# Attention items in the order of query blocks 2, 0, 3, 1, one input chunk turned later, and the last item's transposes moved between out_proj's products

## The chip, the cores and the metric

The kernel runs on one core of one Trainium2 chip. The core has five engines with a queue of instructions each: TensorE (PE in the profile; its weight loads are a row of their own, PEld), VectorE (DVE), ScalarE (ACT), GpSimd (POOL) and SyncE (SP). The metric is the device time of one execution in microseconds (us).

## The reference, cut to what matters

Input x is 512 tokens by 1024 features, float32. Layer A is a gated short convolution and a squared-ReLU MLP; from its output one shared key/value side is projected. Layer B is sparse attention with three branches and a second MLP; a final RMS norm ends it.

```
h = rms_norm(x, norm_mix[0]); b, c, u = split(h @ w_in, 3)
x = x + (b * conv3(c * u)) @ w_out                       # layer A
x = x + square(relu(rms_norm(x) @ w1)) @ w2
k_cmp, v_cmp, k_sel, v_sel, k_win, v_win = shared_kv(rms_norm(x, kv_norm))
q, gates = split(rms_norm(x, norm_mix[1]) @ w_qg)        # layer B
for each query block of 128 tokens, each of 16 heads in 4 groups:
    o_b = softmax(q @ k_b.T + bias, causal) @ v_b        # b = compressed, selected, window
    o = gates[0] * o_c + gates[1] * o_s + gates[2] * o_w
x = x + o @ w_o
x = x + square(relu(rms_norm(x) @ w1)) @ w2
return rms_norm(x, final_norm)
```

With 512 tokens the selected and the window branch both see all earlier keys: block qb of four attends to 128 * (qb + 1) keys in each. The compressed branch has 31 keys.

## The kernel before, in words

Activations lie with features on the partitions, 8 chunks of 128 features by 512 tokens. A product in float32 accuracy is made of three float16 products: every operand is split into a high and a low half (mm3, lines 355 to 358: high by high, high by low, low by high). Weights come from HBM in pieces of up to 1024 columns into a staging tile (wst, 3 buffers), ACT makes the high half (L202), DVE the low half (L203); next_piece (line 215) hands out a piece, and ahead and ahead_fine convert the pieces that follow it. Loads are issued on SP's queue, a piece's load when a staging buffer is free again.

**Start.** x is loaded in four parts of 1, 1, 2 and 2 chunks, with the first weight pieces between them; the last two chunks follow within the first loop. x_chunk (lines 385 to 395) turns a chunk: four transposes on PE (L389) into bank d (even chunks) or e (odd), split by ACT (L303, x0h) and DVE (L304, x0l), and a copy to X by DVE (L394). Seven and later five products on an idle tile (L246) keep PE busy until data is there. The loop from line 418 on works with one weight piece per chunk: chunk c's products for three outputs (pc, pu, pb: two banks each, three products for each, so 18 products of 128x512) and then chunk c + 2 is turned. Ahead of the loop chunks 0 and 1 are turned.

**Attention.** PSUM has banks a, b, c (two of each) and d, e (one of each). An item is a Full (group g, query block qb, branch br, some heads) or a Cmp (the compressed branch for two groups). A Full of block 0 has four heads of 128 keys, of block 1 two of 256, of block 2 one of 384, of block 3 one of 512. So a group has 2, 4, 8 and 8 items in its four blocks, 22 in all, and there are 88 Full and 8 Cmp. An item's stages:

- st0: scores on PE into a bank b (L985, L986); per head, DVE adds the bias and finds the extreme (L993, with a read of the accumulator), ACT takes the exponential (L995, with a read of the sum).
- st1: the probabilities are turned on PE into a bank c (L1001); ACT makes their high half (L1004).
- st2: DVE makes the low half (L1007).
- st3: values on PE into bank d, one bank for all heads and both branches of a block (L1020 to L1022). With a block's last item DVE takes the reciprocal of the sums (L1027), multiplies by the gates (L1028) and scales bank d into o_t (L938); POOL adds the branches up (L940, L943; add_parts).
- st4: where a block has all three branches, finish turns it on PE into a bank c (L954) and ACT and DVE split it into ot (L377, L379).

The loop over i at line 1151 emits st0 of item i, then some background work, then st1 to st4 of items i - 2, i - 3, i - 4 and i - 6. The background generator holds the products that attention still needs (raw keys, queries of groups 1 to 3, the phi network) and out_proj(0), output projection for groups 0 and 1; it is drawn by a credit of 0.65 to 1.03 us an item. Queries of a group are split by ACT (L774) and POOL (L775), four heads. Items stand group by group (line 1128), in a group by blocks 0, 1, 2, 3. Cmp(0, 0) to Cmp(0, 3) stand behind the items 9 to 12 of group 2, Cmp(1, 0), (1, 1), (1, 3), (1, 2) behind the items 3, 7, 11, 15 of group 3. A Cmp whose two groups have both their Full parts is scaled and finished for both at once, else for each by itself.

When the loop ends, the rest of the background runs, then out_proj(2) for groups 2 and 3. Its products over chunks 0 and 1 belong to group 2, those over chunks 2 and 3 to group 3. With early = 2 the first two of the four pairs of outputs do their products over chunks 0 and 1 first. The second MLP follows.

The framework that builds the kernel orders each engine's instructions by itself from the dependences and the order in which they were emitted; issue_after ties a block's instructions on an engine behind a given one.

Of the kernel before, what the change touches and what calls it, by code (L numbers as in the profile page):

```python
# [48 lines left out]
def body(ctx, tc, x, rel_bias, norm_mix, norm_mlp, mlp_w1, mlp_w2, a_w_in, a_conv_w, a_w_out,  # L49
# [176 lines left out]
    def drain(gen):  # L226
        for _ in gen:
            pass
# [126 lines left out]
    def mm3(ps, w, xs, start, stop):  # L355
        PE.matmul(ps, w[0], xs[0], start=start, stop=False)  # L356
        PE.matmul(ps, w[0], xs[1], start=False, stop=False)  # L357
        PE.matmul(ps, w[1], xs[0], start=False, stop=stop)  # L358

    def pair(xs, ps, kn=8, mid=None):  # L360

# [22 lines left out]
    xs = new_split(wk[0], "x0")  # L384

    def x_chunk(c):
        p = bank("de"[c % 2])
        for t in range(4):
            last = PE.transpose(p[:, t * 128:(t + 1) * 128], xt[t][:, c * 128:(c + 1) * 128], ident)  # L389
        if c == 0:  # L390
            with tc.issue_after(last.ins):
                keep_busy(5)
        hi = split_gain(xs, c, p, "mix0")
        DVE.tensor_copy(X[:, c], p)  # L394
        return hi
# [10 lines left out]
    for p in range(4):  # L406
        pc, pu, pb = [], [], []
        if p == 0:
            for dst in (pc, pu, pb):
                dst += [acc(), acc()]  # L410

            def first_pairs(dst, w, c):
                part = 1 if dst is pc else 2 if dst is pu else 0
                for m in range(2):
                    mm3(dst[m], [u[:, part, m * 128:(m + 1) * 128] for u in w], [u[:, c] for u in xs],
                        c == 0, c == 7)

            hi = [x_chunk(0), x_chunk(1)]
            for c in range(6):
                with tc.issue_after(hi[0].ins) if c == 0 else nullcontext():  # L420
                    w = next_piece()
                if c == 0:
                    load_x(6, 8)
                if c == 3:
                    later_vectors()
                for dst in (pc, pu, pb):
                    first_pairs(dst, w, c)
                with tc.issue_after(hi[c + 1].ins):
# [199 lines left out]
    with pool("attn") as ap:  # L628
# [245 lines left out]
        ss2 = SumSq()  # L874
        xm = None

        def out_proj(g, early=0):

            ws, pos_ = [], []

            def products(p, chunks, cv=iter(())):
                for c in chunks:
                    for m in range(2):
                        mm3(pos_[p][m], [u[:, c, m * 128:(m + 1) * 128] for u in ws[p]],
                            [u[:, 2 * g + c] for u in ot], c == 0, c == 3)
                        next(cv, None)
                        yield 0.65

            for p in range(early):
                ws.append(next_piece())  # L890
                pos_.append([abank(), abank()])
                drain(products(p, (0, 1)))
            for p in range(4):
                if p >= early:
                    ws.append(next_piece())
                    pos_.append([abank(), abank()])
                po = pos_[p]
# [44 lines left out]
                for b in range(nb):  # L942
                    POOL.tensor_tensor(dst, dst, t[:, b], op=OP.add)  # L943

        def finish(g, n, qb):

            nonlocal ot
            if ot is None:
                o16 = ap.tile([128, 2, 8, S], F16, name="big", bufs=1)
                ot = (o16[:, 0], o16[:, 1])  # L950
            p = bank("c")
            for j in range(n):
                for i in range(2):
                    PE.transpose(p[:, (2 * j + i) * 128:(2 * j + i + 1) * 128],  # L954
# [10 lines left out]
        class Full:  # L965
# [65 lines left out]
                else:  # L1031
                    self.last = False

            def st4(self):
                if self.last:
                    finish(self.g, 1, self.qb)

        class Cmp:

# [73 lines left out]
            n = max(1, 4 >> qb) if qb < 2 else 1  # L1113
            return [tuple(range(h, h + n)) for h in range(0, 4, n)]

        def full(g):
            return [Full(g, qb, br, hs) for qb in range(4) for br in range(2) for hs in heads_of(qb)]


        def mixed(rest, cmps):  # L1120
# [5 lines left out]
            return out_  # L1126

        items = full(0) + full(1)
        items += mixed(full(2), {9 + qb: Cmp(0, qb) for qb in range(4)})
        items += mixed(full(3), {3: Cmp(1, 0), 7: Cmp(1, 1), 11: Cmp(1, 3), 15: Cmp(1, 2)})  # L1130
        at_item = {11: lambda: load_T(1), 35: lambda: load_T(2), 60: lambda: load_T(3)}
        copy_at = {16: 1, 40: 2, 65: 3}
# [15 lines left out]

        lead = {1: 2, 2: 3, 3: 4, 4: 6}
        credit = 3.0  # L1150
        for i in range(len(items) + 6):
            if i < len(items):
                for k in items[i].need():
                    while k not in done:
# [12 lines left out]
                    credit -= u or 0.1  # L1167
            for s in (1, 2, 3, 4):
                j = i - lead[s]
                if 0 <= j < len(items):  # L1170
                    getattr(items[j], f"st{s}")()
        for _ in bg:
            pass
        lead_in[0] = True
        xm = new_split(work, "xs")
        drain(out_proj(2, 2))
    xs = xm
    ss = ss2

# [156 lines left out]
```

## Time and profile before

| | us |
|---|---|
| median of 3 runs | 1118.34 (1118.34 to 1118.35) |
| the profiled execution | 1118.71 |
| its span, first to last instruction | 1116.9 |
| PE busy in the span | 1091.2 |
| DVE busy | 870.1 |
| ACT busy | 571.0 |
| POOL busy | 58.8 |

The profile is of one execution. A row of a group names line, engine, operation, output<-inputs by the program's names, shapes and count; then the busy time in us, the mean of one in ns, and the idle time of the engine just before them with what ended it. A row of the timeline has the start in us, the duration, engine, line and operation, and in brackets the idle time before it. Matmuls are pipelined: rows overlap, and one's duration is longer than the distance to the next. A row of waits reads "engine line <- what it waited for: us in total, times, longest".

### The profile page before, as it was taken

The page shows a single profiled execution, that of the slowest core. Times are in us where ns is not written, and L with a number is a line of the kernel's source. Part 1 is how long each engine was busy: PE and PEld are TensorE (multiplying, and loading weights), DVE is VectorE, ACT ScalarE, POOL GpSimd, SP SyncE. Part 2 cuts the span into 40 slices and gives each one's busy share as a digit, 9 for nine tenths or more (in the row PEclk, how much of TensorE's full clock was granted, in tenths as well). Part 3 has the DMA queues.
Part 4 walks back from the last instruction along what each step waited for, and adds up shares of the span by engine and source line. Part 5 has one row for each costly group of instructions (what it writes and reads, how often), then busy time and mean ns, then how long its engine had stood idle before and what let it go on. Part 6 is the DMA issues. An engine that isn't in the chain of part 4 may idle for free.

```text
span 1116.9 us, 20043 instructions
## 1 busy us (share of the span) xinstructions
PE 1091.2 (98%) x7960; PEld 693.6 (62%) x7960; DVE 870.1 (78%) x1624; ACT 571.0 (51%) x921; POOL 58.8 (5%) x73
## 2 busy tenths in 40 slices
PE   9999999999999999999998999899999999999996
PEld 4444444446885448875867676675444788445895
DVE  5755466987998667969589879997998798865775
ACT  4532244545343444447678786875655434342352
POOL 1000000000000000000102021311000000000020
PEclk9999999999999999999999999999999999999998
DMA  6433335543333333313333232111653333330321
GB/s 214 127 102 94 113 95 151 149 117 113 114 115 116 104 101 103 106 31 110 116 90 123 84 111 77 39 40 57 180 160 109 105 112 111 114 94 1 95 76 76
DMA packets 149709, 115.75 MB, mean 104 GB/s; under 512 B 8700, under 2 KB 146640, under 8 KB 149616
## 3 DMA queue, kind: packets, MB, share of 16 engines
q1 hardware_dynamic: 146624, 108.88, 32.1%
q10 hardware_dynamic: 2608, 4.97, 1.4%
q8 instruction: 62, 1.02, 0.4%
q0 software_dynamic: 384, 0.63, 0.2%
q14 instruction: 31, 0.25, 0.1%
HBM read 110.22 MB, written 2.14 MB: 101 GB/s over the span
## 4 chain that ended last, share of the span: by engine, by line
PE 89%; DVE 4%; ACT 3%; issue 1%; POOL 1%; DMA 1%; SPq 0%; DVEq 0%; ACTq 0%; POOLq 0%
PE c L572 8%; PE a L572 8%; PE a L356 6%; PE a L357 6%; PE a L358 6%; PE b L358 6%; PE b L357 6%; PE b L356 6%; PE c L357 6%; PE c L356 6%; PE c L358 6%; PE b L572 6%; PE d L572 4%; PE c L1001 2%; PE e L572 2%
## 5 line engine op out<-in xcount | busy, mean ns | idle before, releaser
L202 ACT ACTIVATE whi<-wst 128x1024 f16<-128x1024 f32 (+3 forms) x173 | 144.6, 850 | 180.3 <-PE b L357 64.8
L203 DVE SCALAR_TENSOR_TENSOR wlo<-wst,whi 128x1024 f16<-128x1024 f32 (+3 forms) x173 | 170.9, 996 | 41.7 <-ACT whi L202 41.3
L572 PEld LDWEIGHTS <-whi 128*128 128x128 f16 x1792 | 175.4, 98 | 20.6
L358 PEld LDWEIGHTS <-wlo 128*128 128x128 f16 x1024 | 100.1, 98 | 112.4 <-DVE wlo L203 0.6
L356 PEld LDWEIGHTS <-whi 128*128 128x128 f16 x1024 | 100.4, 98 | 109.6 <-issue 2.7
L357 PEld LDWEIGHTS <-whi 128*128 128x128 f16 x1024 | 100.2, 98 | 108.5 <-issue 2.6
L189 ACT ACTIVATE whi<-wst 128x1792 f16<-128x1792 f32 x64 | 108.4, 1700 | 108.6 <-DVE wst L187 39.6
L190 DVE SCALAR_TENSOR_TENSOR wlo<-wst,whi 128x1792 f16<-128x1792 f32 x64 | 128.9, 2018 | 15.4 <-ACT whi L189 15.4
L187 DVE TENSOR_TENSOR wst<-wst 128x256 f32<-128x256 f32 x256 | 95.3, 421 | 22.1 <-DMA wst<-mlp_w_dram 20.9
L523 DVE TENSOR_TENSOR rl<-ml_z,rh 128x1792 f16<-128x1792 f32 x32 | 64.8, 2024 | 44.7 <-ACT rh L522 44.7
L572 PEld LDWEIGHTS <-wlo 128*128 128x128 f16 x896 | 87.7, 98 | 10.8 <-issue 0.2
L522 ACT ACTIVATE rh<-ml_z 128x1792 f16<-128x1792 f32 x32 | 54.3, 1697 | 67.1 <-DVE ml_z L521 67.1
L995 ACT ACTIVATE at_p<-at_s,at_m 128x128 f32<-128x128 f32 (+3 forms) x128 | 70.7, 553 | 23.3 <-DVE at_m L993 23.0
L358 PE MATMUL b<-xsh,wlo 128*128 128x512 f16 x208 | 78.8, 379 | 0.0
L357 PE MATMUL b<-xsl,whi 128*128 128x512 f16 x208 | 78.8, 379 | 0.0
L356 PE MATMUL b<-xsh,whi 128*128 128x512 f16 x208 | 78.7, 379 | 0.0
L356 PE MATMUL c<-xsh,whi 128*128 128x512 f16 x192 | 72.8, 379 | 0.0
L357 PE MATMUL c<-xsl,whi 128*128 128x512 f16 x192 | 72.8, 379 | 0.0
L358 PE MATMUL c<-xsh,wlo 128*128 128x512 f16 x192 | 72.8, 379 | 0.0
L572 PE MATMUL c<-rl,whi 128*128 128x256 f16 x256 | 69.8, 273 | 0.0
L572 PE MATMUL c<-rh,wlo 128*128 128x256 f16 x256 | 69.8, 273 | 0.0
L572 PE MATMUL c<-rh,whi 128*128 128x256 f16 x256 | 69.8, 273 | 0.0
(314 smaller groups left out, 2544.2 us busy)
## 6 DMA issues: line engine op xcount, KB each, us to landing
wst<-mlp_w_dram SPq DMA_DIRECT2D x256, 256.0 KB, 3.4
wst<-a_w_in_dram SPq DMA_DIRECT2D x18, 512.0 KB, 3.5
wst<-w_kv_dram SPq DMA_DIRECT2D x12, 512.0 KB, 3.6
T<-ext_d ACTq DMA_DIRECT2D x4, 1056.0 KB, 5.8
wst<-a_w_out_dram SPq DMA_DIRECT2D x8, 512.0 KB, 3.5
wst<-b_w_qg_dram SPq DMA_DIRECT2D x8, 512.0 KB, 3.5
wst<-b_w_o_dram SPq DMA_DIRECT2D x8, 512.0 KB, 3.3
wst<-a_w_in_dram SPq DMA_DIRECT2D x7, 384.0 KB, 4.6
```

What stands on the lines that cost most here:

```text
L187: DVE.tensor_tensor(b[:, :, o], b[:, :, x], b[:, :, y], op=e)
L189: ACT.activation(hi, b[:, :, 1:], AF.Copy, scale=sc)
L190: DVE.scalar_tensor_tensor(lo, b[:, :, 1:], sc, hi, op0=OP.mult, op1=OP.subtract)
L202: ACT.activation(hi[:, s:e], w, AF.Copy, scale=sc)
L203: DVE.scalar_tensor_tensor(lo[:, s:e], w, sc, hi[:, s:e], op0=OP.mult, op1=OP.subtract)
L356: PE.matmul(ps, w[0], xs[0], start=start, stop=False)
L357: PE.matmul(ps, w[0], xs[1], start=False, stop=False)
L358: PE.matmul(ps, w[1], xs[0], start=False, stop=stop)
L522: ACT.activation(rh[0][:, p], z[:, 1:8], AF.Copy)
L523: DVE.tensor_tensor(rh[1][:, p], z[:, 1:8], rh[0][:, p], op=OP.subtract)
L572: PE.matmul(acc7[i], wl if n == 1 else wh, xl if n == 2 else xh, stop=c == 7 and n == 2, start=c == 0 and n == 0 and not other, skip_group ...
L995: ACT.activation(self.p[:, w], lg[:, w], AF.Exp, bias=mn[:, j:j + 1], scale=-1.0, accum_out=l[:, br * 4 + h:br * 4 + h + 1])
```

## The change

There are three edits.

1. mm3 and first_pairs return their last product. x_chunk(1) is no longer called ahead of the loop but within its first turn, after the products for pc, and its transposes are tied behind the last of these.
2. full(g) takes an order of blocks, by default 2, 0, 3, 1; group 2 uses 2, 3, 0, 1. The places of the Cmp items in the list and the credits stay.
3. The last item's st4 is taken out of the loop, which is one turn shorter. out_proj(2) is called with early = 3 and calls that st4 between the second and the third early pair, with the transposes going to bank d.

```
-        PE.matmul(ps, w[1], xs[0], start=False, stop=stop)
+        return PE.matmul(ps, w[1], xs[0], start=False, stop=stop)
...
-            hi = [x_chunk(0), x_chunk(1)]
+            hi = [x_chunk(0)]
...
                 for dst in (pc, pu, pb):
-                    first_pairs(dst, w, c)
+                    mm = first_pairs(dst, w, c)
+                    if c == 0 and dst is pc:
+                        with tc.issue_after(mm.ins):
+                            hi.append(x_chunk(1))
...
-        def out_proj(g, early=0):
+        def out_proj(g, early=0, between=None):
...
             for p in range(early):
+                if p == early - 1:
+                    between()
                 ws.append(next_piece())
                 pos_.append([abank(), abank()])
                 drain(products(p, (0, 1)))
...
-        def finish(g, n, qb):
+        def finish(g, n, qb, tag="c"):
...
-            p = bank("c")
+            p = bank(tag)
...
-            def st4(self):
+            def st4(self, tag="c"):
                 if self.last:
-                    finish(self.g, 1, self.qb)
+                    finish(self.g, 1, self.qb, tag)
...
-        def full(g):
-            return [Full(g, qb, br, hs) for qb in range(4) for br in range(2) for hs in heads_of(qb)]
+        def full(g, order=(2, 0, 3, 1)):
+            return [Full(g, qb, br, hs) for qb in order for br in range(2) for hs in heads_of(qb)]
...
-        items += mixed(full(2), {9 + qb: Cmp(0, qb) for qb in range(4)})
+        items += mixed(full(2, (2, 3, 0, 1)), {9 + qb: Cmp(0, qb) for qb in range(4)})
...
-        for i in range(len(items) + 6):
+        for i in range(len(items) + 5):
...
-                if 0 <= j < len(items):
+                if 0 <= j < len(items) and (s, j) != (4, len(items) - 1):
                     getattr(items[j], f"st{s}")()
...
-        drain(out_proj(2, 2))
+        drain(out_proj(2, 3, lambda: items[-1].st4("d")))
```

More of the change, by code (lines that the diff above doesn't have):

```diff
@@ L414, in first_pairs @@
                 for m in range(2):
-                    mm3(dst[m], [u[:, part, m * 128:(m + 1) * 128] for u in w], [u[:, c] for u in xs],
-                        c == 0, c == 7)
-            hi = [x_chunk(0), x_chunk(1)]
+                    mm = mm3(dst[m], [u[:, part, m * 128:(m + 1) * 128] for u in w], [u[:, c] for u in xs],
+                             c == 0, c == 7)
+                return mm
+            hi = [x_chunk(0)]
             for c in range(6):
```

## The prediction

> **What bounds the kernel now.** I read the page's busy times first, then the busy time of each engine by stage, then what TensorE (PE) waited for in the stages where it is not busy throughout.
>
> ```profile
> span 1116.9 us, 20043 instructions
> PE 1091.2 (98%) x7960; PEld 693.6 (62%) x7960; DVE 870.1 (78%) x1624; ACT 571.0 (51%) x921; POOL 58.8 (5%) x73
> ```
>
> PE is the bound: of 1116.9 us it is without work for 25.7. Nothing in the diff removes a product, so the most that any reordering can give back is that idle time, and only where the change reaches it.
>
> ```profile
> 0.00:40.00 40.00, 35.83 (x172) 17.49 (x173) 21.71 (x46) 21.31 (x35) 4.11 (x12) 1.00 0.62 193
> 40.00:555.00 515.00, 515.00 (x3248) 310.34 (x3247) 385.01 (x592) 229.78 (x259) 5.92 (x4) 1.00 0.36 109
> 555.00:652.00 97.00, 92.82 (x980) 64.72 (x979) 82.82 (x234) 75.14 (x211) 10.06 (x11) 1.00 0.33 96
> 652.00:705.00 53.00, 48.92 (x599) 36.47 (x598) 48.28 (x153) 42.20 (x119) 13.00 (x14) 1.00 0.24 80
> 705.00:762.00 57.00, 54.62 (x646) 40.42 (x646) 54.66 (x164) 43.72 (x118) 13.95 (x16) 1.00 0.12 39
> 762.00:790.00 28.00, 26.38 (x168) 13.05 (x167) 20.59 (x34) 14.28 (x26) 3.23 (x4) 1.00 0.25 77
> ```
>
> The columns after the stretch and its length are the busy us (and instructions) of PE, weight loads, DVE, ACT and POOL, then PE's granted clock. PE's idle time is 4.17 us in the first 40, none from 40 to 555 (layer A with its MLP, the key and value projections, the first items), 4.18 in 555:652 (items of groups 0 and 1), 4.08 in 652:705 (group 2 with its four compressed items), 2.38 in 705:762 (group 3), and 1.62 in the change over to out_proj. The clock is 1.00 throughout, so the clock plays no part. DVE is busy 85% of 555:652, but 91% and 96% of the two stretches after it: there DVE leaves PE little that a better order could recover.
>
> **The start.** x's chunk 1 is turned behind the first six products.
>
> ```profile
> 3.92 0.60 SPq L266 DMA_DIRECT2D xt<-x_dram  x1
> 5.21 1.24 PE L246 MATMUL c<-idle 128*128 128x512 f16 x5
> 6.07 1.03 ACT L202 ACTIVATE whi<-wst 128x256 f16<-128x256 f32 x3
> 6.20 0.75 DVE L304 SCALAR_TENSOR_TENSOR x0l<-d,vec,x0h 128x512 f16<-128x512 f32 x1 [4.52 <-ACT x0h L303]
> 7.76 0.63 PE L389 MATMUL e<-ident,xt 128*128 128x128 f32 x4 [1.30 <-DMA xt<-x_dram]
> 8.22 0.38 PE L356 MATMUL a<-x0h,whi 128*128 128x512 f16 x1
> 8.44 0.38 PE L357 MATMUL a<-x0l,whi 128*128 128x512 f16 x1
> 10.41 1.62 DVE L203 SCALAR_TENSOR_TENSOR wlo<-wst,whi 128x256 f16<-128x256 f32 x3
> 12.62 0.38 PE L356 MATMUL a<-x0h,whi 128*128 128x512 f16 x1
> xt<-x_dram SPq DMA_DIRECT2D x1, 512.0 KB, 6.7
> ```
>
> The dummy products end at 6.45, the first third of the weight piece and x0l are there by 6.95, but chunk 0's first product goes at 8.22: PE's queue holds chunk 1's four transposes first, and they wait for x until 7.76. Product follows product by 0.215 us (8.22 to 8.44; the 0.38 of a row overlaps the next). In the built order of the changed kernel nine products stand ahead of those transposes (the diff asks for six; the scheduler puts three of the next pair among them), which gives chunk 0's first product about 6.5, the transposes 6.5 + 9 x 0.215 = 8.45, after their data has landed, and the end of the eighteenth product 6.5 + 18 x 0.215 + 0.46 for the transposes (8.22 less 7.76) = 10.83. Chunk 2's transposes come next; their x, issued at 3.92, lands 6.7 later, at 10.62, just in time. Chunk 1's products, at 12.62 today, could so start at 11.3, 1.3 us earlier. What is late next is DVE: today chunk 1's low half, its copy and the low weights of pieces 0 and 1 are done at 10.41 + 1.62 = 12.03, 4.27 us after the transposes; the built order takes two of piece 0's three small conversions out of that chain (512 of the 1280 columns of the 1.62 us, 0.65), so 8.45 + 3.62 = 12.07. The product that needs it is the fourth of chunk 1 in the new order, at 11.3 + 3 x 0.215 = 11.95. I take off 0.2: **1.1 us gained**. Bounds: 1.77 (8.22 less 6.45) if nothing comes late, 0 if x or a piece lands late. SP's queue moves too: piece 3 is issued when piece 0 is converted, some 2.5 us earlier, and x's last load goes behind it; that one is turned after 30 us, so its delay costs nothing. From 40 to 555 PE never idles, so what is gained at the start is kept.
>
> **The end of attention.** The last item's transposes move behind 24 products of out_proj, and a third pair's twelve follow.
>
> ```profile
> 766.80 0.19 PE L1022 MATMUL d<-VT,at_pl 128*128 128x64 f16 x1
> 767.29 0.68 DVE L938 TENSOR_TENSOR o_t<-d,rl 128x512 f32<-128x512 f32 x1
> 767.89 1.81 DVE L203 SCALAR_TENSOR_TENSOR wlo<-wst,whi 128x512 f16<-128x512 f32 x2
> 768.05 2.23 POOL L943 TENSOR_TENSOR o<-o,o_t 128x256 f32<-128x256 f32 x2 [7.29 <-DVE o_t L938]
> 770.34 0.44 PE L954 MATMUL c<-ident,o 128*128 128x128 f32 x2 [1.62 <-POOL o L943]
> 770.81 0.38 ACT L377 ACTIVATE big<-c 128x256 f16<-128x256 f32 x1 [3.20 <-PE c L954]
> 771.23 0.43 DVE L379 TENSOR_TENSOR big<-c,big 128x256 f16<-128x256 f32 x1 [1.52 <-ACT big L377]
> ```
>
> After the last value product (766.80 + 0.19) the chain scaling, two POOL additions, transposes needs until 770.34, 3.35 us; PE has eight products to fill it and stands for 1.62. The built order puts 24 products there, 24 x 0.215 = 5.16 us, so the chain is covered with 1.8 to spare. The split that follows (770.34 to 771.66, 1.3 us) lies under the third pair's 12 x 0.215 = 2.58. That pair's weights have to be converted earlier than now; in the built order its two halves stand ahead of the last split on both ACT and DVE, directly behind the scaling, so they neither delay it nor arrive late. The transposes take the bank d, whose reader is that same scaling. The gain is the wait, 1.62, and the overlap of a 0.38 row with the next start that the row hides, 0.16: **1.8 us**, bounds 0 and 1.8. If the cover were gone it would be the old wait. The products of pair 0 to 2 now end closer together, 12 products or 2.6 us later for pair 0, and DVE's residuals behind them with them; the MLP's first pair reaches those chunks in the old order, so I cost that at nothing.
>
> **The items.** Each group now takes its query blocks in the order 2, 0, 3, 1 (group 2: 2, 3, 0, 1).
>
> ```profile
> L995 ACT ACTIVATE at_p<-at_s,at_m 128x128 f32<-128x128 f32 x32 | 12.4, 388 | 1.5 <-DVE at_m L993 1.3
> L995 ACT ACTIVATE at_p<-at_s,at_m 128x256 f32<-128x256 f32 x32 | 15.8, 496 | 1.3 <-DVE at_m L993 1.2
> L995 ACT ACTIVATE at_p<-at_s,at_m 128x512 f32<-128x512 f32 x32 | 23.0, 718 | 10.5 <-DVE at_m L993 10.5
> L995 ACT ACTIVATION_READ_ACCUMULATOR at_p<-at_s,at_m 128x1 f32 x128 | 24.1, 188 | 0.0
> L1004 ACT ACTIVATE at_ph<-c 128x512 f16<-128x512 f32 x56 | 32.6, 582 | 6.8 <-PE c L1001 6.6
> 551.05 0.29 DVE L993 CUSTOM_DVE_ANT_0 at_s<-b,T 128x128 f32<-128x128 f32 x1 [0.16 <-PE b L986]
> 604.81 0.63 PE L1001 MATMUL c<-ident,at_p 128*128 128x128 f32 x4 [0.99 <-DVE rl L1027]
> 607.71 0.63 PE L1001 MATMUL c<-ident,at_p 128*128 128x128 f32 x4 [0.99 <-DVE at_pl L1007]
> 611.36 0.38 PE L356 MATMUL a<-xsh,whi 128*128 128x512 f16 x1 [0.71 <-DVE phi_t L834]
> PE b L985 <- POOL Q L775: 0.8, 2, 0.6
> ```
>
> An item of block 0 is four heads of 128 keys and costs ACT 4 x (388 + 188) + 582 ns = 2.89 us; of block 1, two of 256, 1.95; of block 3, one of 512, 1.49; block 2, with 384, less. 96 items in the 211 us from 551 to 762 are one in 2.2. Today a group begins with two items of block 0 and four of block 1: 2 x 2.89 + 4 x 1.95 = 13.6 us of ACT where the beat allows 6 x 2.2 = 13.2, and two block ends on DVE on top. That cluster is at 603 to 612, and there stand three of PE's longest waits, 2.69 us together. In the new order the heaviest six in a row are two of block 0 and four of block 3, 11.7 us, under the beat. The same cluster at group 0 and 2 is covered today by background products, and at group 3 DVE is full anyway. I take the three waits as gone, with 0.16 each that the rows hide: 3.2 us. The first score product of the items is at 551; the last row is group 2's first item, which needs all four heads' low queries from POOL; block 2 comes first now and needs one head: 0.8 gained. Against it: two more compressed items meet groups of which only one is ready, so they are scaled and finished in halves.
>
> ```profile
> L938 DVE TENSOR_TENSOR o_t<-e,rlc 128x512 f32<-128x512 f32 x7 | 4.8, 685 | 0.2 <-DVE at_pl L1083 0.2
> L938 DVE TENSOR_TENSOR o_t<-e,rlc 128x256 f32<-128x256 f32 x1 | 0.4, 425 | 0.4 <-POOL at_p L1068 0.4
> L943 POOL TENSOR_TENSOR o<-o,o_t 128x256 f32<-128x256 f32 x3 | 2.9, 962 | 8.3 <-DVE o_t L938 8.3
> L943 POOL TENSOR_TENSOR o<-o,o_t 128x512 f32<-128x512 f32 x7 | 8.9, 1271 | 25.8 <-DVE o_t L938 25.8
> PE d L1020 <- DVE o_t L938: 1.0, 2, 0.7
> ```
>
> Two halves cost DVE 2 x 425 - 685 = 165 ns more, the split of the finished block about as much, for two items 0.66 us in a stretch where DVE is 96% busy: 0.7 lost. **Net 3.3 us gained**, bounds +10.6 (all idle time of 555:762) and -9 (rival 4).
>
> **The sum**: 1.1 + 1.8 + 3.3 = 6.2 us. The profiled execution took 1118.71, 1.8 around its span; less 6.2 that is 1112.5. The median, 1118.34, is 0.37 below it, so I forecast **1112.1**, and 1110 to 1114 for this case alone.
>
> [...]
>
> **Rivals.** [...] Chance 0.06. (2) DVE sets the pace of all items, and the waits only move: its 91 and 96% speak for it, its 85% in 555:652 against. Then the start and the end remain, 2.9 us: 1115.4. Chance 0.18. (3) The even mix frees more: all 4.18 of 555:652, half of the 6.46 after it, and the hidden 0.16 of some 15 waits, 9.8, with the 2.9 12.7 in all: 1105.6, or up to 1109 if only part of it comes. For it speaks that the waits on at_pl and on the bank c are short and follow bursts. Chance 0.14. (4) Slower: the single bank d. A block's first value product waits until the block before it has been scaled out of d. Two such waits show today (last row, 0.7 the longest). Block 0 now stands between two long ones; the scaling then has to pass DVE's queue within the 2.2 us of one item. Its own three operations take 1.03, so from two other operations of 0.6 queued ahead of it the wait appears. If all 16 block ends paid 0.85 (0.69 and the hidden 0.16), that is 13.6 less the 1.3 paid now: 1112.1 + 12.3 = 1124.4. Chance 0.12. (5) The start is eaten by landings and the items gain nothing: 1116.5 to 1118. Chance 0.06. That the change doesn't do what it says is excluded by the built order, read engine by engine.
>
> **How the numbers follow.** Forecast 0.44, the others as given. A measurement of this kernel tells 0.2%, 2.2 us, from no change. Below 1116.1 lie the forecast, (1), (3) and most of (2): faster 0.78; (5) and the rest of (2): same 0.10; (4): slower 0.12. The range runs from within (3) to within (5): 1106.5 to 1117, which leaves out (4) and half of (3).
>
> **What would show it.** Right: first product near 6.5 and chunk 1's near 11.5; no wait before the transposes on d; idle PE in the items near 7 us instead of 10.6; POOL's Q wait gone. Wrong: waits of d's first value products on o_t at many block ends (4), or the same idle time at other places with DVE busier (2). The forecast falls if the item stretch, from the first score product to the first out_proj product on c, isn't shorter by 2 us or more.

## The result, and the profile after

Before 1118.70 us, after **1116.37 us** (medians of 22 executions each, on one chip): ratio 0.9979 [0.9972, 0.9985], 2.3 us faster where 6.2 were forecast. The interval runs from 1.7 to 3.1 us, on both sides of the 2.2 us that the prediction gives as what a measurement can tell from no change. The 22 executions before lie within 1118.20 to 1119.16, those after within 1114.74 to 1118.13: the changed kernel scatters more than three times as widely. The profiled execution of after took 1115.42, 0.95 below the median. One execution of one experiment (e10 below) took 1149.32 us in a slow state and stands in no number here.

The page's first lines, and the busy time by stage, with the stretches moved with the work (columns as in the prediction; lines of the kernel are 4 higher behind the start, 6 higher in the items):

```profile
span 1113.6 us, 20039 instructions
PE 1091.4 (98%) x7960; PEld 693.9 (62%) x7960; DVE 869.5 (78%) x1627; ACT 571.7 (51%) x922; POOL 58.5 (5%) x75
```
```profile
0.00:40.00 40.00, 37.22 (x176) 18.40 (x177) 21.66 (x46) 21.46 (x36) 4.11 (x12) 1.00 0.64 194
545.00:652.00 107.00, 102.97 (x1136) 72.46 (x1134) 87.88 (x252) 84.54 (x229) 9.70 (x11) 1.00 0.36 100
652.00:705.00 53.00, 49.06 (x618) 37.29 (x618) 48.61 (x147) 43.16 (x117) 14.54 (x16) 1.00 0.23 74
705.00:760.00 55.00, 53.31 (x617) 38.57 (x617) 53.28 (x168) 41.66 (x120) 11.05 (x16) 1.00 0.16 50
760.00:790.00 30.00, 29.82 (x186) 14.92 (x184) 22.59 (x37) 15.71 (x28) 4.69 (x6) 1.00 0.27 77
790.00:1114.00 324.00, 314.01 (x2138) 209.27 (x2135) 255.05 (x404) 143.69 (x156) 8.52 (x12) 0.99 0.34 102
```

PE has the same work (1091.4 against 1091.2) in a span 3.3 shorter. The change over to out_proj is full now (0.18 idle where 1.62 stood). The item stretches still have 4.03, 3.94 and 1.69 idle, 9.7 in all; the forecast said 7, before were 10.6.

Three marks divide the 3.3 us: the first score product of the items came at 550.40 and comes at 549.82; the last value product at 766.80 and 764.80. So 0.6 came ahead of the items, 1.4 in them, and the remaining 1.3 behind them. Group by group (a group runs from its first score product to the next group's; the last one to the last value product), first before, then after:

```profile
550.40:599.88 49.48, 48.53 (x498) 33.34 (x495) 39.54 (x116) 39.25 (x105) 7.15 (x7) 1.00 0.32 92
599.88:655.21 55.33, 52.08 (x572) 36.78 (x569) 46.70 (x133) 43.49 (x122) 5.21 (x6) 1.00 0.41 123
655.21:712.10 56.89, 50.94 (x623) 37.52 (x621) 52.49 (x159) 45.27 (x127) 16.58 (x17) 1.00 0.18 57
712.10:766.80 54.70, 54.19 (x645) 39.58 (x642) 52.61 (x160) 40.09 (x110) 8.07 (x11) 1.00 0.16 50
```
```profile
549.82:599.43 49.61, 48.33 (x497) 33.49 (x493) 38.49 (x113) 39.70 (x104) 6.42 (x6) 1.00 0.32 88
599.43:654.51 55.08, 52.02 (x571) 36.60 (x568) 47.40 (x137) 43.55 (x124) 5.63 (x7) 1.00 0.44 127
654.51:709.99 55.48, 50.63 (x623) 37.67 (x621) 52.27 (x159) 45.25 (x125) 15.52 (x17) 1.00 0.19 59
709.99:764.80 54.81, 54.15 (x645) 39.28 (x642) 53.11 (x164) 39.98 (x113) 9.18 (x14) 1.00 0.16 50
```

The second number is the length. Groups 0 and 1, where the forecast saw the cluster of waits, are 0.12 shorter together; group 2 is 1.41 shorter; group 3 is as long as before.

### The profile page after: what moved, and what is told of

Its sections match the earlier page's. It is cut to its first block, busy times and chain, and to the rows that moved or that the text cites. A ratio compares the mean times of both kernels' runs of the same rounds, so it can differ in the third digit from the quotient of the medians.

```text
span 1113.6 us, 20039 instructions
## 1 busy us (share of the span) xinstructions
PE 1091.4 (98%) x7960; PEld 693.9 (62%) x7960; DVE 869.5 (78%) x1627; ACT 571.7 (51%) x922; POOL 58.5 (5%) x75
## 4 chain that ended last, share of the span: by engine, by line
PE 86%; DVE 7%; ACT 3%; issue 2%; POOL 1%; DMA 0%; DVEq 0%; ACTq 0%; SPq 0%
PE c L576 8%; PE a L576 8%; PE a L357 6%; PE a L356 6%; PE a L358 6%; PE b L576 6%; PE c L357 6%; PE c L358 6%; PE c L356 6%; PE b L358 6%; PE b L357 5%; PE b L356 5%; PE d L576 4%; PE e L576 2%; PE c L1007 2%
## 5 line engine op out<-in xcount | busy, mean ns | idle before, releaser
L1001 ACT ACTIVATE at_p<-at_s,at_m 128x384 f32<-128x384 f32 (+3 forms) x128 | 70.8, 554 | 21.4 <-DVE at_m L999 20.5
```

The lines of the kernel that those rows point to most:

```text
L1001: ACT.activation(self.p[:, w], lg[:, w], AF.Exp, bias=mn[:, j:j + 1], scale=-1.0, accum_out=l[:, br * 4 + h:br * 4 + h + 1])
```

## The experiments

Sixteen experiments ran, in groups of four, each group beside the kernel before on the same chip (its medians there: 1118.62, 1118.83, 1118.65, 1118.61). A ratio's interval is some 1 us to each side, so differences below that are read from the traces, not from the medians alone. "Low clock" counts the executions whose granted clock, averaged over the span, was 0.996 or less. That mark is close: every profile also has half clock in its last 4.3 to 7.6 us (0.50 from 1109.04 to the end at 1113.64 in after, from 1110.61 to 1116.93 in before), so the mean of e16's profile, with full clock in between, is 0.9966 and that of e2's, with a fall in the middle, 0.9956.

| kernel | median us | ratio to before | least and most | low clock |
|---|---|---|---|---|
| e1 start edit alone | 1117.89 | 0.9994 [0.9985, 1.0002] | 1116.98, 1118.70 | 0 of 11 |
| e2 order alone | 1118.56 | 1.0000 [0.9991, 1.0009] | 1117.00, 1120.30 | 8 of 11 |
| e3 end edit alone | 1117.82 | 0.9993 [0.9984, 1.0002] | 1117.41, 1118.23 | 0 of 11 |
| e4 start and end | 1117.33 | 0.9989 [0.9980, 0.9998] | 1116.77, 1118.25 | 0 of 11 |
| after (first comparison) | 1116.37 | 0.9979 [0.9972, 0.9985] | 1114.74, 1118.13 | 13 of 22 |
| e5 after again | 1116.50 | 0.9979 [0.9969, 0.9989] | 1115.10, 1117.90 | 5 of 8 |
| e6 after, 9 idle products more | 1116.40 | 0.9978 [0.9969, 0.9987] | 1115.39, 1117.15 | 0 of 11 |
| e7 after, DVE eased | 1113.90 | 0.9956 [0.9942, 0.9970] | 1112.96, 1114.47 | 3 of 4 |
| e8 before, DVE eased | 1116.72 | 0.9980 [0.9971, 0.9989] | 1115.72, 1116.97 | 1 of 10 |
| e9 new order in group 2 alone | 1117.45 | 0.9990 [0.9981, 0.9998] | 1116.08, 1118.80 | 10 of 11 |
| e10 compressed items 3 earlier | 1117.04 | 0.9986 [0.9977, 0.9995] | 1116.14, 1118.19 | 0 of 10 |
| e11 norm's products later | 1116.79 | 0.9980 [0.9971, 0.9989] | 1115.40, 1118.01 | 5 of 11 |
| e12 e10 and e11 | 1115.84 | 0.9975 [0.9965, 0.9984] | 1115.06, 1117.10 | 0 of 10 |
| e13 group 2 in the old order | 1117.87 | 0.9994 [0.9985, 1.0003] | 1117.54, 1118.45 | 0 of 11 |
| e14 group 2 as 2, 0, 3, 1 | 1117.08 | 0.9985 [0.9977, 0.9994] | 1116.22, 1117.68 | 0 of 11 |
| e15 compressed items 1 earlier, and e11 | 1117.60 | 0.9989 [0.9980, 0.9997] | 1116.41, 1118.23 | 5 of 11 |
| e16 e4 and e11 | 1117.69 | 0.9990 [0.9981, 0.9999] | 1116.51, 1118.10 | 0 of 11 |

The kernel before had a low clock in 2 of 122 executions beside them.

### Each edit alone (e1 to e4)

Each takes its part of the change's diff and nothing else; in short, e1, e2 and e3 (e4 has e1's and e3's):

```
-            hi = [x_chunk(0), x_chunk(1)]
+            hi = [x_chunk(0)]
...
+                        with tc.issue_after(mm.ins):
+                            hi.append(x_chunk(1))
```
```
-        def full(g):
+        def full(g, order=(2, 0, 3, 1)):
...
+        items += mixed(full(2, (2, 3, 0, 1)), {9 + qb: Cmp(0, qb) for qb in range(4)})
```
```
-        drain(out_proj(2, 2))
+        drain(out_proj(2, 3, lambda: items[-1].st4("d")))
```

> Only the first edit (chunk 1 turned behind chunk 0's first products). Forecast: 1.1 us faster than the kernel before. By the trace of the changed kernel, in which the first product came at 7.10 instead of 6.5 because the dummy products ran at half pace for 1.5 us longer, and in which everything after the start was 0.6 us earlier: 0.6 us faster, and 1.1 in an execution whose products reach full pace as early as in the profile of before. Rival 5 (eaten by landings): 0 to 0.2.

> Only the second edit (the order of the query blocks). Forecast: 3.3 us faster. Rival 2 (DVE paces the items, waits only move): 0, within 0.5 either way. By the trace of the changed kernel, in which first score product to last value product took 1.4 us less: 1.4 faster. Rival 4 (single bank d): slower.

> Only the third edit (last item's transposes between the early pairs, three early pairs). Forecast: 1.8 us faster. By the trace of the changed kernel, in which the wait before the transposes is gone but the norm ahead of the second MLP waits 0.5 for the last sums: 1.1 to 1.3 faster, and such a wait of about 0.5 on the sums of squares stands in its profile.

> The first and the third edit, blocks in the old order. Forecast: 2.9 us faster than before, so 3.3 slower than the changed kernel would have been; if the order of blocks is worth nothing, the same time as the changed kernel (2.3 us faster than before); if it costs something, faster than the changed kernel.

The start alone gave 0.7, the end alone 0.8, both 1.3; the order alone nothing. (These are medians. The intervals of e1 and e3 include no change, that of e4 doesn't.) The start's gain was mis-sized twice. First, the profile of before was a late execution: x's chunk 1 was turned at 7.76 there, but at 7.35 in the trace of e2, 7.43 in that of e3 and 7.33 in that of e8, which have the old start. Second, the rows of after:

```profile
4.60 1.11 PE L389 MATMUL d<-ident,xt 128*128 128x128 f32 x4
5.51 1.75 PE L246 MATMUL c<-idle 128*128 128x512 f16 x5
7.10 0.38 PE L356 MATMUL a<-x0h,whi 128*128 128x512 f16 x1
11.42 0.60 PE L389 MATMUL d<-ident,xt 128*128 128x128 f32 x4
11.86 0.38 PE L356 MATMUL a<-x0h,whi 128*128 128x512 f16 x1
```

The same five dummy products took 1.75 where they took 1.24, the four transposes 1.11 instead of 0.66: PE started at half pace (0.427 from product to product) and came to full pace (0.215) 1.85 us later than in the profile of before (at 6.54 instead of 4.69 by the trace's record of the granted clock). Before, such a delay hid under the wait for x (in e8, with the old start, full pace came at 6.88 and the first product at 7.77); now the first product stands right behind the dummies, so it showed: 7.10 instead of 6.5. In e4 full pace came early (its last two dummies took 0.59 together, from 5.74) and the first product at 6.40; there chunk 2's transposes, at 11.18, waited for x:

```profile
11.18 0.66 PE L389 MATMUL d<-ident,xt 128*128 128x128 f32 x4 [0.28 <-DMA xt<-x_dram]
```

So either the pace or x's landing holds this start. Chunk 2's transposes came at 11.78, 11.86 and 12.19 with the old start (e2, e3, before) and between 10.85 and 11.74 with the new one, latest in e15, where full pace came latest (7.08).

### What the end edit gave back (e3, e11, e16)

In the traces of after, e3 and e4 nothing waits at the last item's transposes. Instead, ahead of the second MLP:

```profile
PE d L352 <- DVE ssacc L346: 0.5, 1, 0.5
```

That is the norm's sum over partitions, waiting for DVE's last sum of squares. DVE's first residual and its last sum, before and then after:

```profile
776.21 0.69 DVE L487 SCALAR_TENSOR_TENSOR X<-c,X 128x512 f32<-128x512 f32 x1 [4.55 <-PE c L358]
...
794.93 0.68 DVE L346 TENSOR_TENSOR ssacc<-ssacc,sq 128x512 f32<-128x512 f32 x1
```
```profile
774.97 0.69 DVE L491 SCALAR_TENSOR_TENSOR X<-c,X 128x512 f32<-128x512 f32 x1 [3.69 <-PE c L358]
...
792.46 0.70 DVE L346 TENSOR_TENSOR ssacc<-ssacc,sq 128x512 f32<-128x512 f32 x1
```

Counted from the last value product (766.80, 764.80) the first residual now comes at 10.17 instead of 9.41: pair 0 ends 12 products later (2.58) and the wait of 1.78 is gone, which would make 0.80; 0.76 was measured. From there to the last sum DVE's queue is nearly without a gap (busy for 19.20 of the 19.40 us of 776.21:795.61 before, for 18.07 of the 18.19 of 774.97:793.16 after). PE gained 1.78, but the last sum comes only 0.47 sooner after the last value product (27.66 instead of 28.13). e11 and e16 move the norm's products six products back in PE's queue:

```
-            if c == 5 and mid:
+            if c == 6 and mid:
```

> The changed kernel with the four small products of each MLP's norm six products later in the queue of TensorE. In the changed kernel they wait 0.5 us for the last sum of squares, which DVE reaches through a queue that is full from the first residual on. If that wait is what the end edit gave back: 0.5 to 0.6 us faster than the changed kernel, and no wait on the sums in its profile. If DVE's chain sets the end of that stretch anyway: no difference, the wait comes back at the row tile.

> The kernel with the first and third edit, old order, with the norm's products six later. If DVE's full queue from the first residual on sets when the second MLP gets its row factors, the wait only moves to the transposes that spread them (as in the changed kernel with this edit): within 0.3 of 1117.3. If the wait on the sums was avoidable: 0.5 to 0.6 less, 1116.8.

Neither is faster than the kernel it was made from by anything that can be told. In e16 the wait on the sums is gone, and there stands in its place, at the transposes that spread the row factors:

```profile
PE e L327 <- DVE rs_r L320: 0.7, 1, 0.7
```

So that stretch is paced by DVE, and the wait only has a choice of places. From the last value product to the end of the span it is 350.1 us in before, 349.3 in e3, 349.5 in e4, 349.1 in e5 and 348.8 in after: the end edit is worth 0.6 to 1.3 of its 1.8. The wait of 0.5 tells part of what is missing; the rest, and why it differs, stays open.

### Is it DVE in the items? (e7, e8)

In these two kernels the background products of the items leave out the low halves of their weights, so their results are not the reference's:

```
...
+            light = LIGHT[0] <= i < LIGHT[1]
+            lo = hi if light else wpool.tile([128, PIECE], F16, name="wlo", bufs=NW)
...
+                if not light:
+                    DVE.scalar_tensor_tensor(lo[:, s:e], w, sc, hi[:, s:e], op0=OP.mult, op1=OP.subtract)
```

> The changed kernel, in which the weights of the items' background products (queries of groups 1 to 3, raw keys, phi, out_proj of groups 0 and 1) have no low half: the high half stands in its place, so TensorE has the same products and DVE about 32 us less in the item stretch of 215 us. Rival 2 (DVE sets the pace of all items): the waits of TensorE there, about 13 us with what the rows hide, shrink by half or more: 6 to 10 us faster than the changed kernel, 1106 to 1110. If TensorE's waits are the dependences of single items and bursts, not DVE's load: less than 3 us faster, 1113 to 1116.

> The kernel before with the same lightening of DVE. Under rival 2 the order of blocks matters only where DVE is not full, so with DVE eased the two orders should differ by the forecast 3 us: this 1112 to 1114 where the changed kernel comes to 1106 to 1110 (of the difference about 1.3 to 2 is start and end). If the order itself is worth nothing even with DVE eased: the difference is only the 1.3 to 2 us of start and end.

Some 22 us less DVE work within the item stretch (191.3 to 169, where 32 less were expected) bought 2.1 us with the old order and 2.6 with the new one, not 6 to 10: DVE does not set the pace of all items. But it does in the cluster. Groups 0 and 1 with DVE eased, old order (e8), then new (e7):

```profile
549.95:599.33 49.38, 48.57 (x498) 33.20 (x493) 32.49 (x103) 39.29 (x105) 6.82 (x7) 1.00 0.33 91
599.33:653.53 54.20, 51.73 (x571) 36.75 (x568) 39.41 (x121) 43.58 (x122) 5.21 (x6) 1.00 0.43 123
```
```profile
549.49:598.33 48.84, 47.94 (x497) 33.51 (x493) 31.75 (x101) 39.81 (x104) 6.08 (x6) 1.00 0.32 90
598.33:651.38 53.05, 51.68 (x572) 36.62 (x569) 39.59 (x124) 43.41 (x123) 5.63 (x7) 1.00 0.43 127
```

103.58 against 101.89: with DVE eased the new order is worth 1.7 us here, with DVE loaded 0.12, by one profile of each kernel. (Over all four groups these two profiles are alike, 213.66 and 213.74; e7's has 6.83 us of half clock in groups 2 and 3, e8's none.) The two rows of 600 to 612, before and after, tell why (DVE is the third busy time, ACT the fourth):

```profile
600.00:612.00 12.00, 9.31 (x133) 8.10 (x130) 11.55 (x47) 11.00 (x41) 0.72 (x1) 1.00 0.59 199
```
```profile
600.00:612.00 12.00, 9.60 (x117) 7.01 (x115) 11.95 (x34) 10.45 (x34) 1.44 (x2) 1.00 0.77 241
```

The new order did take load off ACT there (11.00 to 10.45), as meant. DVE was the fuller engine already, and is full throughout now; PE is idle for 2.69 us of these 12 before and 2.40 after. PE's waits in 545:652 of after are all on DVE:

```profile
PE d L1026 <- DVE o_t L944: 0.9, 2, 0.7
PE b L991 <- DVE at_m L999: 0.9, 2, 0.5
PE a L356 <- DVE at_s L797: 0.8, 2, 0.5
PE c L1007 <- DVE at_pl L1013: 0.6, 1, 0.6
...
```

The 0.12 is a sum of two parts, as the other profiles show. Group 1 takes 55.3 us in all six profiles with the old order there and DVE loaded, and 55.1 in all ten with the new one. Group 0 takes 49.5 in the six and 49.6 to 50.7 in the ten, with waits for DVE (o_t 0.2 to 0.5, at_pl up to 0.7) that come and go: the new order costs time there, in two profiles over 1 us.

### Why the time scatters: half pace at 707 us (e2, e5, e6)

e2's profile is of an execution in which group 2 took 56.98 with the same order that took 55.48 in the profile of after. The two run alike up to 707 us. Then, in e2 (the number behind POOL's busy time is the granted clock):

```profile
702.00:706.00 4.00, 1.56 (x20) 1.17 (x19) 2.76 (x10) 3.90 (x8) 2.73 (x3) 1.00 0.00 0
706.00:707.00 1.00, 0.76 (x4) 0.22 (x3) 1.00 (x2) 0.97 (x5) 0.93 (x2) 1.00 0.00 0
707.00:711.00 4.00, 3.83 (x24) 2.95 (x24) 3.08 (x10) 2.35 (x9) 1.67 (x2) 0.57 0.01 4
711.00:715.00 4.00, 4.00 (x51) 3.04 (x50) 3.59 (x10) 3.02 (x9) 0.73 (x1) 1.00 0.42 131
```

The 0.57 over four us is a clock of one half (0.50 in 708:710) for 2 x (1 - 0.57) x 4 = 3.4 us, in which PE does 1.7 us of work. In e5's profile the same 3.4 us lie between 705 and 709, and those of e7, e9 and e11 show it at the same point of the work (mean clock of the execution 0.995, 0.994 and 0.996), for twice as long in e7 and e9 (6.83; the clock is 0.95 over e7's 702.68:763.23 and 0.94 over e9's 654.17:711.98). These five are all that was seen directly; of the other executions only the mean clock is known. Ahead of it PE has little to do: the last items of group 2 are its two light blocks, no background product is left until out_proj can begin, and two long waits stand 2.8 us apart (e2):

```profile
703.30 0.63 PE L954 MATMUL c<-ident,o 128*128 128x128 f32 x4 [1.09 <-DVE at_pl L1007]
...
706.10 0.38 PE L356 MATMUL a<-big,whi 128*128 128x512 f16 x1 [1.45 <-ACT big L377]
```

To compare kernels, I slid a window of 3.4 us, the length of e2's fall, over PE's rows from 545 to 790 and kept the place with the least busy time; the row of that place in before, e14 and after:

```profile
704.60:708.00 3.40, 1.80 (x32) 1.38 (x31) 3.08 (x7) 3.30 (x8) 2.49 (x3) 1.00 0.00 0
```
```profile
702.60:706.00 3.40, 1.85 (x24) 1.61 (x25) 2.11 (x7) 3.30 (x8) 1.96 (x2) 1.00 0.00 0
```
```profile
702.00:705.40 3.40, 1.36 (x19) 1.17 (x19) 2.16 (x8) 3.30 (x8) 2.33 (x3) 1.00 0.00 0
```
All kernels of the table with a low clock in a third of their executions or more (after, e2, e5, e7, e9, e11, e15) have their emptiest place at 1.30 to 1.39 (in e7 and e9 partly within the fall itself, ahead of it 1.55 and 1.57); all others, e6 and e10 among them, at 1.76 or more. The traces show the halving (0.50), its length (3.41 us in e2, e5 and e11, 6.83 in e7 and e9) and the chance in it (a low clock in 5 of 8 executions of e5, in 13 of 22 of after). They also show that PE was not idle ahead of it: in e2 it was busy for 1.36 of the 3.40 us from 702.20 to 705.60, 40%, and no single gap ahead of its fall was longer than 1.45 us.

The times of the falls have a pattern. In the record of the granted clock, each of the five falls begins a whole number of steps of 3.413 us after full pace came at the start: e2 206 steps (4.01 to 707.15), e5, e9 and e11 205, e7 204. The step can be read from two other profiles: the half clock of the last microseconds begins 1102.50 us after full pace in after (6.54 to 1109.04) and 1105.92 in before (4.69 to 1110.61), 323 and 324 steps of 3.413; and the falls last one step or two. From these times I infer that the busy time in fixed windows of this length counts, and not the emptiest place. The windows of this grid that end at the fall in e5 and in e2, and the emptiest one of the grid in after, whose clock stayed:

```profile
701.94:705.35 3.41, 1.36 (x18) 1.17 (x19) 2.18 (x8) 3.31 (x8) 2.40 (x3) 1.00 0.00 0
```
```profile
703.73:707.15 3.42, 1.73 (x20) 0.92 (x18) 2.18 (x8) 3.35 (x8) 3.19 (x4) 1.00 0.00 0
```
```profile
702.86:706.27 3.41, 1.72 (x19) 1.26 (x20) 2.17 (x9) 3.31 (x6) 3.20 (x3) 1.00 0.00 0
```

In e11, e7 and e9 the window ahead of the fall held 1.35, 1.49 and 1.54. The profile of after has the same lull as e5's, but two windows of its grid share it; full pace came 0.92 us later at its start (6.54, 5.62). By these profiles, whether the lull costs the clock hangs on when full pace came, which differs from profile to profile (3.99 to 7.08 us); no experiment tested this.

The experiment against it puts products into the lull, e6:

```
...
+                if i in (68, 69):
+                    with tc.issue_after(items[i].mm.ins):
+                        fill = bank("a") if i == 68 else fill
+                        for _ in range(5 if i == 68 else 4):
+                            PE.matmul(fill, KD[:, 0, 0, 0, :128], KD[:, 0, 0, 0, :512], start=True, stop=True)
```

> The changed kernel once more, unchanged, as the measure for the three that run beside it, with a second profile. If its spread (1114.7 to 1118.1, against 1.3 us of the kernel with the first and third edit) comes from TensorE falling to half pace at about 707 us in a part of the executions, as in the profile of the kernel with the second edit alone: again 1116 to 1117 with a spread of 2 us or more, and executions whose mean granted clock is 0.998 lie at 1115 to 1116, those at 0.996 or below above 1116. If the spread has another cause: no tie between clock and time.

> The changed kernel with nine products more of 128x512 on a bank that nobody reads, five and four of them put where TensorE waits between about 702 and 706 us (ahead of the transposes of a finished block, and ahead of out_proj's first product). They compute nothing that is used. Theory of the pace: TensorE is then busy enough there, never falls to half pace, and the executions that today lose 1.5 us don't: median 1115.0 to 1116.0, spread as narrow as that of the old order, granted clock 0.998 in nearly all. If idle time has nothing to do with it: the median as that of the changed kernel or up to 0.9 us slower (the four products at the second place that don't find a wait, 4 x 0.215), the same spread.

The theory's sign came as expected: with nine idle products there, no execution of e6 has a low clock (5 of 8 beside it), and the slowest fell from 1117.90 to 1117.15. Its size did not: the median is the same; that the nine products cost about what they save fits this, but was not measured apart. In after and e5 together the 12 executions at 0.997 or 0.998 have a median of 1115.5, the 18 at 0.996 or less one of 1116.8. The clock is not all of the scatter: kernels without a low clock spread from 0.8 us (e3) to 2.0 (e10, e12).

### Which group, and can the lull be filled? (e9, e10, e12 to e15)

The edits to the changed kernel, e9, then e13 (e14 has full(2) there, so the default order), then e10 (e12 has e11's edit beside it; e15 has it too, with 8 + qb):

```
-        def full(g, order=(2, 0, 3, 1)):
+        def full(g, order=(0, 1, 2, 3)):
```
```
-        items += mixed(full(2, (2, 3, 0, 1)), {9 + qb: Cmp(0, qb) for qb in range(4)})
+        items += mixed(full(2, (0, 1, 2, 3)), {9 + qb: Cmp(0, qb) for qb in range(4)})
```
```
-        items += mixed(full(2, (2, 3, 0, 1)), {9 + qb: Cmp(0, qb) for qb in range(4)})
+        items += mixed(full(2, (2, 3, 0, 1)), {6 + qb: Cmp(0, qb) for qb in range(4)})
```

> The changed kernel with the new order in group 2 alone (2, 3, 0, 1); groups 0, 1 and 3 go back to 0, 1, 2, 3. The forecast put most of the items' gain into groups 0 and 1 (the waits at 603 to 612, 3.2 us): without them about 3 us slower than the changed kernel. By the traces, in which the steps of the score products show groups 0 and 1 0.1 us shorter, group 3 unchanged and group 2 1.4 shorter where TensorE keeps its pace: within 0.4 us of the changed kernel, and the drop to half pace stays in a part of the executions.

> The changed kernel with group 2 in its old order (0, 1, 2, 3); groups 0, 1 and 3 keep the new one. If the order is worth something in group 2 alone (1.4 us less when TensorE keeps its pace) and the drop to half pace comes from group 2's order: 1117.0 to 1117.5, as the kernel with the first and third edit alone, with its narrow spread and a granted clock of 0.997 or 0.998 in all. If groups 0 and 1 gain what the forecast said: 1114 to 1115.

> The changed kernel with group 2 in the order of the others (2, 0, 3, 1), so that the last items of group 2 are block 3, then block 1, and block 0 stands earlier. If the drop needs the two light blocks 0 and 1 side by side ahead of out_proj's first product: no drop, clock 0.997 or 0.998, 1115.0 to 1116.0. If the lull has its cause in the missing background work alone: drops as in the changed kernel, 1116 to 1117.5.

> The changed kernel with the four compressed items of groups 0 and 1 three items earlier (behind items 6 to 9 of group 2), so that out_proj of groups 0 and 1 becomes ready some 6 us earlier and has products for the stretch at 702 to 706. Theory of the pace: no drop to half pace in any execution, granted clock 0.998 or 0.997 in all, and the waits there filled by work that is needed: 1113.5 to 1115.5. If DVE sets the pace there (rival 2), the products only change places: 1115.3 to 1116.5, with a narrow spread; if the lull comes back elsewhere, the same median and spread as the changed kernel.

> The changed kernel with the compressed items three items earlier and the norm's products six later. If both theories hold: 2 to 3 us faster than the changed kernel, 1113 to 1114.5, with a spread below 2 us; if only the one on the norm: 0.5 faster.

> The changed kernel with the compressed items of groups 0 and 1 one item earlier and the norm's products six later in the queue. If one item of background work is enough against the drop and costs less at the end than three: 1114.5 to 1115.5, clock 0.997 or 0.998. If not: 1116 to 1117 with the wide spread.

With the new order in groups 0, 1 and 3 alone (e13) the time is 1117.87, no better than with none of it (e4, 1117.33), and no clock is low. With it in group 2 alone (e9) it is 1117.45, no better either, but there 10 of 11 had a low clock, and the one that had not took 1116.08. So that the gain lies in group 2 is read from the traces (56.9 us with the old order in e3, 55.48 in after), not shown by a median; that group 2's order makes the lull is shown by the low clocks, which are gone in e13. I had expected e9 within 0.4 us of the changed kernel; it is 1 us above. e14, with block 0 away from block 1, has no drop, but its median is 0.7 above the changed kernel (1117.08), within the interval. e10 fills the lull with work that is needed, and the drop is gone in all executions; but group 2 then carries more products (57.5 us), the item stretch of its profile is 217.4, and two waits of 0.6 return in the change over, where that work is missing: 1117.04, slower than expected. Of the 217.4, 0.95 more than in after lie in group 0 (50.56), far ahead of the items that the edit moves. Together with the later norm (e12) it came to 1115.84, the lowest median of all that compute the reference, with no low clock; beside the changed kernel that is 0.5, within the intervals, so it beats the kernel before (ratio 0.9975) and is at best a little ahead of the change. e15 shifts by one item: the lull stays (5 of 11).

## Why the prediction was wrong, point by point

**The bound.** PE is the bound, and its busy time did not change: right. "The clock is 1.00 throughout, so the clock plays no part" is a step that failed. It holds in the row, but the row says nothing of how near the clock is to falling. The change moved waits together, and the mean clock was 0.996 or less in 18 of 30 executions of the changed kernel, against 2 of 122 of the kernel before.

**The start** was forecast at 1.1 and gave 0.7 by the medians, 0.6 between the two profiles. The mechanism was right (first product ahead of chunk 1's transposes). Too early was the term "chunk 0's first product about 6.5": it took the pace of one execution for granted, and the product came at 7.10. With 7.10 in its place the same sum gives 11.9 for chunk 1's products, and they came at 11.86. And 12.62, from which the gain was counted, belongs to an execution whose x came 0.3 to 0.4 late against e2, e3 and e8. The gain was kept, as the step said.

**The end** was forecast at 1.8. The wait went entirely, as computed, and the third pair did cover the split. The step that failed is "I cost that at nothing": the residuals that begin later (0.80 by the same arithmetic of 12 products, 0.76 measured) push DVE's chain, and the MLP's norm waits 0.5 for it. What remained is 0.8 by e3's median and trace, 0.6 to 1.3 by the traces of e4, e5 and after.

**The items** were forecast at 3.3, and this is the term that made the forecast wrong: 1.4 in the profile of after, 0.2 in that of e2, and about 1 by the medians (after against e4). The failing step is the cluster: "I take the three waits as gone" (3.2). I had counted ACT's load there, 13.6 against a beat of 13.2, and not DVE's, which was 11.55 of 12 us and is 11.95 now, although the three rows that I quoted name DVE as what ended each wait (rl, at_pl, phi_t). The cluster is DVE's, so the waits changed their names (o_t, at_m, at_pl) and their sum hardly: 2.69 us before, 2.40 after between 600 and 612. That DVE is the cause, e7 and e8 show, by one profile each: with DVE eased the same order gains 1.7 in groups 0 and 1. POOL's Q wait went from 0.8 to 0.5, not to nothing:

```profile
PE b L991 <- POOL Q L779: 0.5, 2, 0.3
```

What group 2 gained lies in waits that I had not named. The waits listed there sum to 5.6 us before (nine of them) and 4.3 after (ten); the longest of before, then of after:

```profile
PE c L1001 <- DVE big L379: 0.9, 1, 0.9
PE c L1076 <- DVE at_pl L1083: 0.9, 1, 0.9
...
```
```profile
PE a L356 <- ACT big L377: 1.4, 1, 1.4
PE c L960 <- DVE at_pl L1013: 1.3, 2, 1.1
...
```

Less in sum, but the two longest are longer, and next to each other: that is the lull in which the clock falls. Group 3, where I took off 0.7 for halved compressed items, is as long as before (54.70, 54.81).

**The rivals.** (2), DVE sets the pace and the waits only move, was the nearest: its 1115.4 is 1.0 from the median, and it names what happened in the cluster and at the end. In the strong form, for all items, it fell with e7 and e8. (4), the bank d: such waits are 0.9 in 545:652, 0.7 the longest, against a total of 1.0 in the items' waits quoted before; one in group 0 (o_t, 0.2 to 0.5) is new with the order, but there is no sign of sixteen. (1), with 0.06, counted on more work for POOL: its busy time did not grow (58.8, 58.5), and no run shows what more of it would cost. (5) is wrong on the items' side for group 2, but its landing was seen in e4. None had the clock.

**The range** held the time (1106.5 to 1117); the forecast's own range (1110 to 1114) did not. The last mark for a wrong forecast was badly chosen: the third edit itself moves out_proj's first product on c ahead of the transposes (770.61 before, 764.83 after), so to that product the stretch is 5.2 shorter. Up to the last value product, which the edit does not move, it is 1.4 shorter, not 2.

**What stays open.** Why the gain of group 2 is not seen in e2's or e9's median, though in after's, is only partly told by the low clocks (8 of 11, 10 of 11, and 18 of 30). Where exactly the clock falls, no run tells: a window of the grid with 1.73 busy fell (e2), one with 1.72 did not (after).

## What to carry to other kernels

Before calling a burst one engine's, read the busy time of every engine in that burst's own window: here the reordering took ACT from 11.00 to 10.45 of 12 us, and PE's waits stood on DVE (11.55, then 11.95), 2.69 us before and 2.40 after. Ask of work that is moved closer together who consumes it next, even off the bound engine: 2.6 us of delay for pair 0 gave back 0.5 of the 1.8 us that the end edit won. And look at the bound engine's emptiest few microseconds: with waits side by side PE lost half its clock here, for 3.41 or 6.83 us in five profiles and with a low clock in 18 of 30 executions, so a kernel that scatters more than before deserves a look at the granted clock.

## What the runs showed of the hardware

TensorE's clock fell to half (0.50 in e2's 708:710) for 3.41 or 6.83 us in the middle of a kernel in which it is 98% busy, after windows of 3.41 us in which it was 40 to 51% busy (1.35 to 1.73 us in e11, e5, e7, e9 and e2). All five falls began 204 to 206 whole steps of 3.413 us after full pace came at the start; the half clock at the end began 323 (after) and 324 (before) such steps behind it. Kernels whose emptiest 3.4 us are 52% busy or more had a mean clock of 0.996 or less in hardly any execution (2 of 122 of the kernel before, 1 of 10 of e8, none of the others). In after and e5 the executions with a low clock took 1.3 us more in the median. At the start full pace came between 3.99 (e14) and 7.08 us (e15) in eighteen profiles with the same dummy products ahead of it.
